# A hybrid decoder trunk: places, ring and order for the weights of the pooling mixer's seven half products

## The chip, the core and the metric

The kernel runs on one core of one Trainium2 chip. A core has five engines that run side by side, each through its own list of instructions in order: TensorE (PE; its weight loads are shown apart as PEld), VectorE (DVE), ScalarE (ACT), GpSimd (POOL) and SyncE (SP). Here SP issues nearly all plain DMAs, and POOL those that add onto what is already in the target. The metric is the device time of one execution in microseconds (us); times inside an execution are counted from the start of its span.

## What is computed

Two residual layers over 512 tokens of width 1024, each a token mixer and a SwiGLU feed-forward network (FFN), and a last norm. Layer 0 mixes by causal pooling, layer 1 by dilated windowed attention. The change touches the pooling mixer, above all its output projection by `w_out`:

```python
def pool_mixer(h, w_in, w_group, scale, w_out):
    u = einsum('bsd,de->bse', h, w_in)                    # 512x1024 by 1024x1024
    outs = [(cumsum(u_g) - lagged by w) / count - u_g for u_g, w in the 4 groups]
    z = einsum('bsgc,gce->bsge', outs, w_group) * scale   # four 256x256
    return einsum('bsd,de->bse', z, w_out)                # 1024x1024

x = x + pool_mixer(rmsnorm(x), ...)
x = x + swiglu(rmsnorm(x), ...)
```

## The kernel before

**Precision.** Each operand is held as two parts, `hi` and `lo`. ACT casts (`hi`), DVE subtracts (`lo`, "the rest"), and a product is three matmuls: hi by hi, hi by lo, lo by hi.

**Weights.** All weights stand in one `queue` in the order of use. `weights(i, ...)` loads raw tiles ahead (512 KB each, `wraw`, five in turn) and casts some items ahead into a ring of five pairs `whi`/`wlo` (pool `wspl`, `RING = 5`). An item with `"pool": "b"` gets its pair (`bhi`/`blo`) from another pool, which is opened only after the windows of the mixer, in memory that the `poolu` tiles held until then. An item with `"sums"` is loaded into a tile of the pool `s` (`sraw`), opened at the same place.

**The seven half products.** Where `SEVEN_OUT[0]` is on (it is; `SEVEN_OUT[1]`, for attention, is off), the output projection is one level of Strassen-Winograd: seven products of half matrices in place of eight. Product `i` takes a left operand `u` (quarters of `z`, or sums and differences of them, split into hi and lo by the class `Left`) and a right one, a quarter of `w_out` or a sum of quarters. It has 24 matmuls of 512 columns, ordered by weight tile (z = 0, 1), then token block (t = 0, 1), then chunk (c = 0, 1), three for each. Sums of weights are made by POOL's adding DMAs: the tile for product 1 gets two quarters, then a third is added for product 2, then a fourth for product 5, each after the cast before it has read the tile. `SEVEN` is the order in which they run: 0, 1, 2, 5, 4, 3, 6. Products 0, 2, 4 and 6 accumulate in the PSUM pair `p`, 1 and 5 in `r`, 3 in `q`, and `flush` adds a finished sum into the stream `x` on DVE.

**Around them.** `group_products(0)` and `(1)` make `z`, and ACT evicts their banks into `raw` (L744). The second half runs between product 0 and product 1 (`after_first`). `Left.behind` is called after a product and makes left operands of later ones. `norm.square`, `norm.gained` and `norm.prepare` make the normed rows of the FFN, `turned_rows` transposes the first 128-row blocks on PE (L401), and then product 6 runs, t = 0 first. The FFN starts with products `("one", 0, 0)`, `(0, 3)`, `(1, 0)`, `(1, 3)`, then i = 1 and 2 for both groups; their weights with i = 1, 2, 5 are sums in `vraw` tiles. `late` makes its `t` operands from the last token blocks.

**Order.** PE's order is that of the code. For the other engines a scheduler orders the recorded instructions by its own costs; blocks marked `high_priority(URGENT)` go first. `issue_after` ties an instruction behind another. SP and POOL keep the order of the code too. Each list is fixed when the kernel is built, so an instruction that waits holds all that stand behind it on its engine.

Of the kernel before, what the change touches and what calls it, by code (L numbers as in the profile page):

```python
# [17 lines left out]
P = 128  # L18
# [52 lines left out]
SEVEN = (0, 1, 2, 5, 4, 3, 6)  # L71
# [7 lines left out]
def trunk_kernel(ctx: ExitStack, tc: tile.TileContext, x_in, xT, gam, gains, consts, ident_d, w0, wT, w1, wv, w_down, out):  # L79
# [49 lines left out]
    def load(i):  # L129
# [27 lines left out]
    def weights(i, split_ahead=4, load_ahead=5, held=0):  # L157

        load_ahead = queue[i].get("ahead", load_ahead)
        for n in range(loaded["w"], min(len(queue), i + load_ahead)):  # L160
# [5 lines left out]
        load_sums()  # L166
        while len(ready) < min(loaded["w"], i + split_ahead):
# [36 lines left out]
    j_in.append([enqueue(w0[i], (2, S)) for i in range(4, 8)])  # L204
    w_out, wo = (rows_of(wT[i]) for i in range(2))

    def enqueue_seven(w, order, then=None):
# [295 lines left out]
    class Left:  # L503
# [6 lines left out]
        def split(self, u, src, ks=(slice(0, 4),)):  # L510
            hi, lo = self.places[u]
            for k in ks:
                split(hi[:, k, :], lo[:, k, :], src[:, k, :])
# [33 lines left out]
        def reserve(self):  # L547

            if 4 not in self.places:
                self.places[4] = [  # L550
                    wspl.tile([P, 1024], F32R, name=name).rearrange("p (k s) -> p k s", k=4) for name in ("whi", "wlo")
                ]

    def seven_projection(js, left, norm, shift, p, r, q, tps, after_first, keep):
# [5 lines left out]
        def operands(i):  # L560
            return [weights(j, split_ahead=6, held=z + (i in (4, 3, 6))) for z, j in enumerate(js[i])]

        def products(i, ws, ts=range(2)):
            hi, lo = left.places[(0, 1, 2, 3, 6, 5, 4)[i]]
            places = [(z, t, c) for z in range(2) for t in ts for c in range(2)]
# [16 lines left out]
        def product(i):  # L582
# [1061 lines left out]
```

## Time and profile before

| | us |
|---|---|
| three runs before | 1007.15, 1008.66, 1009.75 (median 1008.66) |
| the profiled execution, its own time | 1008.38 |
| its span, first to last instruction | 1006.6 |
| mean granted clock of TensorE in it | 0.987 |
| product 0 starts | 63.06 |
| product 6 ends and the FFN starts | 130.23 |

Rows of the timeline read: start, duration, engine, source line, operation, output <- inputs, shape, and in brackets the idle time of the engine just before and what ended it. Rows of waits read: who waited for whom, us in total, times, longest. Rows of stretches give busy time by engine. "mm", "early" and "pair" are PSUM banks.

### The profile page before, as it was taken

To read this page: it belongs to the slowest core of one execution; us is meant where nothing else is said; L and a number is where in the kernel's file an instruction comes from. 1 tells how busy PE (TensorE), PEld (TensorE's weight loads), DVE (VectorE), ACT (ScalarE), POOL (GpSimd) and SP (SyncE) were. 2 spreads that over 40 slices of the span, in tenths; PEclk is the share of its full clock that TensorE was granted. 3 is DMA by queue.
4 is the path that set the end of the run, shared out by engine and by line. 5 is a ranking of instruction groups with operands and counts; after the bars stand their busy time and mean duration, and the time that the engine had idled before them with its cause. 6 is when DMAs were issued, how large, how long until landed. Compare 5 with 4: busy or idle time off the path is not lost.

```text
span 1006.6 us, 15596 instructions
## 1 busy us (share of the span) xinstructions
PE 976.2 (97%) x6004; PEld 863.9 (86%) x6004; DVE 800.3 (80%) x1097; ACT 589.9 (59%) x919; POOL 134.3 (13%) x132
## 2 busy tenths in 40 slices
PE   9996998899999999999999999999999999999997
PEld 7874788898898899888888899889998898899886
DVE  6445987989798888879887747669989788888877
ACT  5544856564675566657354454447655566566655
POOL 0101101001001110110212104100001101111110
PEclk9997998999999999999999999999999999999999
DMA  9745777648946987665332128924757966897652
GB/s 334 215 127 87 214 153 214 146 127 205 255 118 174 252 203 189 148 157 186 100 103 61 53 79 245 216 46 149 195 139 199 246 169 147 225 235 179 156 129 112
DMA packets 82186, 168.24 MB, mean 167 GB/s; under 512 B 6256, under 2 KB 6640, under 8 KB 82112
## 3 DMA queue, kind: packets, MB, share of 16 engines
q1 hardware_dynamic: 59088, 123.09, 37.4%
q0 software_dynamic: 22736, 43.89, 25.6%
q8 instruction: 47, 0.77, 0.3%
q14 instruction: 27, 0.22, 0.1%
q10 hardware_dynamic: 288, 0.27, 0.1%
HBM read 165.09 MB, written 2.13 MB: 166 GB/s over the span
## 4 chain that ended last, share of the span: by engine, by line
PE 80%; ACT 0%; DVE 0%; issue 0%; ACTq 0%
PE pair L888 31%; PE pair L1032 21%; PE mm L299 4%; PE mm L301 3%; PE mm L300 3%; PE pair L914 3%; PE p L914 2%; PE r L914 1%; PE mm L1485 1%; PE mm L1486 1%; PE mm L1487 1%; PE mm L460 1%; PE mm L461 1%; PE mm L462 1%; PE mm L1532 1%; PE mm L914 1%
## 5 line engine op out<-in xcount | busy, mean ns | idle before, releaser
L183 DVE TENSOR_TENSOR wlo<-wraw,whi 128x1024 fp32r<-128x1024 f32 (+2 forms) x190 | 221.8, 1172 | 56.4 <-ACT whi L179 56.0
L179 ACT CAST whi<-wraw 128x1024 fp32r<-128x1024 f32 (+2 forms) x189 | 183.9, 979 | 133.8 <-PE pair L888 28.6
L179 ACT CAST whi<-vraw 128x1024 fp32r<-128x1024 f32 (+1 forms) x108 | 105.2, 979 | 118.3 <-DVE vraw L185 39.9
L183 DVE TENSOR_TENSOR wlo<-vraw,whi 128x1024 fp32r<-128x1024 f32 (+1 forms) x108 | 121.5, 1133 | 46.4 <-ACT whi L179 46.3
L888 PE MATMUL pair<-h,whi 128*128 128x512 f32 (+1 forms) x640 | 143.2, 349 | 0.0
L888 PEld LDWEIGHTS pair<-h,whi 128*128 128x128 f32 x640 | 109.1, 189 | 13.4
L888 PE MATMUL pair<-t,whi 128*128 128x512 f32 (+1 forms) x512 | 110.6, 337 | 0.0
L1032 PE MATMUL pair<-whi,u_hi 128*128 128x512 f32 (+1 forms) x284 | 109.9, 387 | 0.0
L1032 PE MATMUL pair<-wlo,u_hi 128*128 128x512 f32 (+1 forms) x284 | 109.9, 387 | 0.0
L1032 PE MATMUL pair<-whi,u_lo 128*128 128x512 f32 (+1 forms) x284 | 109.7, 386 | 0.0
L888 PEld LDWEIGHTS pair<-t,whi 128*128 128x128 f32 x512 | 86.0, 190 | 8.4
L888 PE MATMUL pair<-h,wlo 128*128 128x256 f32 x512 | 89.2, 281 | 0.0
L888 PEld LDWEIGHTS pair<-h,wlo 128*128 128x128 f32 x512 | 76.1, 188 | 4.2
L185 DVE TENSOR_TENSOR vraw<-vraw,wraw 128x1024 f32<-128x1024 f32 (+1 forms) x66 | 75.2, 1139 | 0.7
L888 PE MATMUL pair<-t,wlo 128*128 128x256 f32 x384 | 71.9, 282 | 0.0
L144 POOL DMA_DIRECT2D wraw<-w x22 | 26.5, 1206 | 323.5 <-DMA wraw<-w 144.8
L299 PE MATMUL mm<-h,whi 128*128 128x512 f32 (+1 forms) x176 | 64.3, 365 | 0.0
L301 PE MATMUL mm<-h,wlo 128*128 128x512 f32 (+1 forms) x176 | 63.4, 360 | 0.0
L300 PE MATMUL mm<-h,whi 128*128 128x512 f32 (+1 forms) x176 | 63.4, 360 | 0.0
L1032 PEld LDWEIGHTS pair<-whi,u_lo 128*128 128x128 f32 x284 | 53.3, 188 | 10.9
L1032 PEld LDWEIGHTS pair<-whi,u_hi 128*128 128x128 f32 x284 | 53.4, 188 | 10.4
L1032 PEld LDWEIGHTS pair<-wlo,u_hi 128*128 128x128 f32 x284 | 53.4, 188 | 10.2
(413 smaller groups left out, 2063.8 us busy)
## 6 DMA issues: line engine op xcount, KB each, us to landing
wraw<-w SPq DMA_DIRECT2D x116, 512.0 KB, 4.5
wraw<-w_down SPq DMA_DIRECT2D x32, 512.0 KB, 4.1
vraw<-w SPq DMA_DIRECT2D x22, 512.0 KB, 5.0
wraw<-w POOLq DMA_DIRECT2D x22, 512.0 KB, 6.9
vraw<-w POOLq DMA_DIRECT2D x22, 512.0 KB, 9.2
wraw<-wT SPq DMA_DIRECT2D x16, 512.0 KB, 4.2
vraw<-w_down POOLq DMA_DIRECT2D x12, 512.0 KB, 7.1
wraw<-w_down SPq DMA_DIRECT2D x24, 256.0 KB, 3.3
```

Of the source, the lines that this page charges most:

```text
L144: nc.gpsimd.dma_start(dst, more, accum_op=ALU.add)
L179: nc.scalar.copy(hi[:, :n], raw[:, :n])
L183: nc.vector.tensor_sub(lo[:, :n], raw[:, :n], hi[:, :n].bitcast(F32))
L185: nc.vector.tensor_add(raws[into][:, :n], raws[into][:, :n], raws[more][:, :n])
L299: nc.tensor.matmul(ps, lhsT=whi, rhs=xhi, start=first, stop=False, **kw)
L300: nc.tensor.matmul(ps, lhsT=whi, rhs=xlo, start=False, stop=False, **kw)
L301: nc.tensor.matmul(ps, lhsT=wlo, rhs=xhi, start=False, stop=last, **kw)
L460: nc.tensor.matmul(ps, lhsT=xhi, rhs=w[0][:, k, :], start=first, stop=False)
L461: nc.tensor.matmul(ps, lhsT=xhi, rhs=w[1][:, k, :], start=False, stop=False)
L888: mat = lambda o, w, m, **kw: nc.tensor.matmul(o, lhsT=w, rhs=m, skip_group_check=True, **kw)
L914: nc.tensor.matmul(ps[:, g, :], lhsT=w[:, g, c, :], rhs=right[:, z, c, :], start=i in (0, 1, 3) and g + c + k == 0, stop=c == 3 and k == 2 ...
L1032: nc.tensor.matmul(acc(t), lhsT=u, rhs=w, start=first, stop=n == len(places) - 1, skip_group_check=True)
```

## The change

Five things, all of them in the first mixer.

1. The two tiles for weight sums (`sum0`, `sum1`) are allocated with the mixer's first tiles. `load_until` loads them and, with them, all items to the end of product 1, right after the window bands are loaded. Behind them the load-ahead goes on, so that product 4's raw tiles and their adding DMAs are early too.
2. The weights of products 0 and 1 with z = 1 take the ring, not pool `b`.
3. The casts of the weights of products 2 and 5 are tied behind the last eviction of the group products (`cast_behind`); `group_products(1)` casts no more than its own weights ahead.
4. The order becomes 0, 1, 2, 4, 5, 3, 6. `behind` makes left operands in another sequence, only its first step stays URGENT, and `reserve` goes. Norm squares of the second half now come before product 5, those of the first before product 3.
5. The transposes move from ahead of product 6 to behind its first six matmuls, and the rests of the turned rows with them.

```diff
-SEVEN = (0, 1, 2, 5, 4, 3, 6)
+SEVEN = (0, 1, 2, 4, 5, 3, 6)
...
-            raw = pools["s"].tile([P, 1024], F32, name="sraw")
+            raw = pools["s"]()
...
+    def load_until(end):
+
+        for n in range(loaded["w"], min(len(queue), end)):
             if queue[n].get("sums") and "s" not in pools:
                 break
             if queue[n]["kind"] == "w":
                 load(n)
             loaded["w"] = n + 1
         load_sums()
...
-                item = dict(kind="w" if src else "sum", shape=(2, S), rows=True, ahead=8, **({"pool": "b"} if z else {}))
+                item = dict(kind="w" if src else "sum", shape=(2, S), rows=True, ahead=8, **({"pool": "b"} if z and i > 1 else {}))
...
-            with tc.high_priority(URGENT):
-                if i is None:
+            if i is None:
+                with tc.high_priority(URGENT):
                     self.next_sum(FIRST)
                     self.split(2, self.spare)
-                    self.split(5, more[:, :, FIRST])
-                    nc.vector.tensor_sub(t[:, :, FIRST], more[:, :, FIRST], t[:, :, FIRST])
-                elif i == 0:
-                    self.split(6, t[:, :, FIRST])
-                elif i == 1:
-                    self.split(3, more[:, :, SECOND])
-                    self.next_sum(SECOND)
-                elif i == 4:
-                    self.split(4, self.spare)
...
+            elif i == 0:
+                nc.vector.tensor_sub(t[:, :, FIRST], more[:, :, FIRST], t[:, :, FIRST])
+                self.split(6, t[:, :, FIRST])
+            elif i == 1:
+                self.split(5, more[:, :, FIRST])
+                self.next_sum(SECOND)
+            elif i == 2:
+                self.split(3, more[:, :, SECOND])
+                self.split(4, self.spare)
...
-        product(5)
+        product(4)
+        ws = operands(5)
+        for b in range(2):
+            norm.square(b, 1)
+            norm.gained(b, 1)
+        product(5, ws)
         for b in range(2):
             norm.square(b, 0)
             norm.gained(b, 0)
-        left.reserve()
-        product(4)
-        for b in range(2):
-            norm.square(b, 1)
-            norm.gained(b, 1)
             norm.prepare(b)
         product(3)
         for t in range(2):
             norm.square(2 + t, 0, q[t])
-        rests = turned_rows(norm, shift, list(enumerate(tps())))
         ws = operands(6)
-        rests()
+        products(6, ws, (0,), (0,))
+        turned_rows(norm, shift, list(enumerate(tps())))()
+        products(6, ws, (0,), (1,))
         for t in range(2):
+            if t:
+                products(6, ws, (1,))
             norm.gained(2 + t, 0)
-            products(6, ws, (t,))
             flush(6, t)
...
+            sums = [pm.tile([P, 1024], F32, name=f"sum{i}") for i in range(2)]
...
+            pools["s"] = lambda: sums.pop(0)
+            load_until(j_out[1][-1] + 1)
...
-            whi, wlo = weights(j_grp[half])
+            whi, wlo = weights(j_grp[half], 1 if half else 4)
...
-                group_products(1, early)
+                made = group_products(1, early)
+                for i in (2, 5):
+                    for j in j_out[i]:
+                        queue[j]["cast_behind"] = made.ins
                 left.second()
                 left.behind(None)
```

The diff also changes lines of the attention layer that act only with `SEVEN_OUT[1]` on, and gives one item of `j_in` a load-ahead of 8.

Three places of the fixed order, each before and after. First ACT around the evictions of the group products; `early` and `mm` are PSUM banks, `wraw_304` (before) and `wraw_306` (after) hold product 0's weights with z = 1, `sraw` and `sum` the weight sums. Before, from the split of the last window bank on:

```order
L422 CAST p_hi_109<-early3_105 128x512
L179 CAST bhi_610<-wraw_304 128x1024
L179 CAST whi_618<-sraw_604 128x1024
L744 ACTIVATE raw1_107<-early0_102,g_sb_76 128x512
L179 CAST bhi_623<-sraw_607 128x1024
L744 ACTIVATE raw1_107<-early1_103,g_sb_76 128x512
```

In the changed kernel these casts stand earlier, around the first half's evictions:

```order
L183 CAST whi_528<-wraw_300 128x1024
L183 CAST whi_532<-wraw_306 128x1024
L183 CAST whi_536<-wraw_308 128x1024
L705 ACTIVATE u_hi_116<-mm_501,r4_341 128x512
L183 CAST whi_618<-sum0_109 128x1024
L747 ACTIVATE raw0_106<-mm_540,g_sb_76 128x512
L747 ACTIVATE raw0_106<-mm_548,g_sb_76 128x512
L426 CAST h_74<-raw0_106 128x512
L747 ACTIVATE raw0_106<-mm_558,g_sb_76 128x512
L183 CAST whi_623<-sum1_110 128x1024
L747 ACTIVATE raw0_106<-mm_566,g_sb_76 128x512
```

The casts of products 0 and 1 have moved from ahead of and among the evictions of the second group half (`raw1`) to ahead of and among those of the first (`raw0`), and they go to `whi`, not `bhi`.

Second, DVE from the last eviction of the group products to the rests of product 2's weights (`wlo_629`, `blo_634` before; `wlo_695`, `blo_700` after). `x<-x,mm` is a flush of product 1. Before:

```order
L526 SCALAR_TENSOR_TENSOR spare_sum_108<-spare_sum_108,raw1_107 128x1024
L423 TENSOR_TENSOR h_74<-raw1_107,h_74 128x1024
L538 TENSOR_TENSOR raw0_106<-raw1_107,raw0_106 128x4x256
L423 TENSOR_TENSOR h_74<-spare_sum_108,h_74 128x1024
L580 TENSOR_TENSOR x_72<-x_72,mm_602 128x512
L423 TENSOR_TENSOR p_lo_110<-raw0_106,p_hi_109 128x1024
L580 TENSOR_TENSOR x_72<-x_72,mm_603 128x512
L423 TENSOR_TENSOR p_lo_110<-raw1_107,p_hi_109 128x1024
L526 SCALAR_TENSOR_TENSOR spare_sum_108<-spare_sum_108,raw1_107 128x1024
L183 TENSOR_TENSOR wlo_629<-sraw_604,whi_628 128x1024
L183 TENSOR_TENSOR blo_634<-sraw_607,bhi_633 128x1024
```

And in the changed kernel, to the flush of product 2 (`x<-mm,x`):

```order
L530 SCALAR_TENSOR_TENSOR spare_sum_108<-spare_sum_108,raw1_107 128x1024
L542 TENSOR_TENSOR raw0_106<-raw1_107,raw0_106 128x4x256
L187 TENSOR_TENSOR wlo_695<-sum0_109,whi_694 128x1024
L427 TENSOR_TENSOR h_74<-spare_sum_108,h_74 128x1024
L577 TENSOR_TENSOR x_72<-x_72,mm_613 128x512
L577 TENSOR_TENSOR x_72<-x_72,mm_614 128x512
L427 TENSOR_TENSOR p_lo_112<-raw0_106,p_hi_111 128x1024
L187 TENSOR_TENSOR blo_700<-sum1_110,bhi_699 128x1024
L187 TENSOR_TENSOR wlo_705<-wraw_615,whi_704 128x1024
L187 TENSOR_TENSOR blo_709<-wraw_628,bhi_708 128x1024
L575 TENSOR_TENSOR x_72<-mm_611,x_72 128x512
L575 TENSOR_TENSOR x_72<-mm_612,x_72 128x512
```

Product 2's first rest has moved from the tenth place to the third, its second from the eleventh to the eighth; the flush of product 2, which product 4 on the same bank needs, stands behind both rests of product 4's weights.

Third, DVE near the end of the stage, around the rest of product 6's second weights (`blo_837` before, `blo_830` after), whose raw tile is the next one that SP loads for the FFN ahead of the `vraw` tiles. `x<-x,mm` is the flush of product 4, `x<-early,x` that of product 3. Before:

```order
L183 TENSOR_TENSOR blo_793<-wraw_752,bhi_792 128x1024
L578 TENSOR_TENSOR x_72<-mm_603,x_72 128x512
L368 TENSOR_TENSOR even_rows_593<-x_72,gain_595 128x512
L361 TENSOR_SCALAR ss_594<-ss_594 128x1
L183 TENSOR_TENSOR wlo_799<-wraw_758,whi_798 128x1024
L368 TENSOR_TENSOR odd_rows_81<-x_72,gain_595 128x512
L361 TENSOR_SCALAR ss_594<-ss_594 128x1
L183 TENSOR_TENSOR blo_837<-wraw_790,bhi_836 128x1024
L580 TENSOR_TENSOR x_72<-x_72,mm_600 128x512
```

And in the changed kernel:

```order
L187 TENSOR_TENSOR wlo_798<-wraw_753,whi_797 128x1024
L379 TENSOR_TENSOR v1_884<-ss_608 128x1
L380 RECIPROCAL r1_886<-s1_885 128x1
L381 TENSOR_SCALAR v1_872<-v1_872,r1_874,s1_873 128x1
L381 TENSOR_SCALAR v1_884<-v1_884,r1_886,s1_885 128x1
L382 RECIPROCAL r1_874<-v1_872 128x1
L575 TENSOR_TENSOR x_72<-early0_102,x_72 128x512
L382 RECIPROCAL r1_886<-v1_884 128x1
L575 TENSOR_TENSOR x_72<-early1_103,x_72 128x512
L187 TENSOR_TENSOR blo_830<-wraw_789,bhi_829 128x1024
```

The rest of product 6's second weights has moved from ahead of the flush two products before it to behind the flush of product 3, the last before it.

More of the change, by code (lines that the diff above doesn't have):

```diff
@@ L166, in weights @@
         load_sums()
+    def weights(i, split_ahead=4, load_ahead=5, held=0):
+        load_ahead = queue[i].get("ahead", load_ahead)
+        load_until(i + load_ahead)
         while len(ready) < min(loaded["w"], i + split_ahead):
@@ L203, in trunk_kernel @@
     j_in = [[enqueue(w0[0][:, i * S : (i + 1) * S], (1, S)) for i in range(2)] + [enqueue(w0[i], (2, S)) for i in range(1, 4)]]
-    j_in.append([enqueue(w0[i], (2, S)) for i in range(4, 8)])
+    j_in.append([enqueue(w0[i], (2, S), **({"ahead": 8} if i == 7 else {})) for i in range(4, 8)])
     w_out, wo = (rows_of(wT[i]) for i in range(2))
@@ L512, in split @@
             for k in ks:
[L513 removed]
+                self.cast = split(hi[:, k, :], lo[:, k, :], src[:, k, :])[0]
         def first(self, k):
@@ L560, in operands, with products @@
         def operands(i):
-            return [weights(j, split_ahead=6, held=z + (i in (4, 3, 6))) for z, j in enumerate(js[i])]
-        def products(i, ws, ts=range(2)):
+            return [weights(j, split_ahead=6, held=z) for z, j in enumerate(js[i])]
+        def products(i, ws, ts=range(2), zs=range(2)):
             hi, lo = left.places[(0, 1, 2, 3, 6, 5, 4)[i]]
-            places = [(z, t, c) for z in range(2) for t in ts for c in range(2)]
+            places = [(z, t, c) for z in zs for t in ts for c in range(2)]
             for z, t, c in places:
@@ L580, in flush, with product @@
                     nc.vector.tensor_sub(at, at, accs[i][t])
-        def product(i):
-            products(i, operands(i))
+        def product(i, ws=None):
+            products(i, ws or operands(i))
             for t in range(2):
@@ L743, in group_products @@
                         with tc.high_priority(URGENT):
-                            nc.scalar.activation(raw[half][:, 2 * gg + m, :], ps, AF.Copy, scale=sc)
+                            made = nc.scalar.activation(raw[half][:, 2 * gg + m, :], ps, AF.Copy, scale=sc)
                             if half == 0 and m == 1:
@@ L751, in group_products @@
                     )
+            return SEVEN_OUT[0] and made
         quarters = lambda t: t.rearrange("p a b -> p (a b)").rearrange("p (u k s) -> p u k s", u=4, k=4)
@@ L1182, in trunk_kernel @@
         at = 8 * SPAN
-        angles = aw.tile([P, D], F32, name="angles", bufs=1)
+        seven = SEVEN_OUT[1]
+        angles = (ap if seven else aw).tile([P, D], F32, name="angles", bufs=1)
         cosr, sinr = (angles[:, cs] for cs in COLS)
@@ L1501, in trunk_kernel @@
         mp = actx.enter_context(tc.tile_pool(name="merged", bufs=1, reuse_waits="tile"))
-        seven = SEVEN_OUT[1]
         pools["b"] = actx.enter_context(tc.tile_pool(name="wob", bufs=3 if seven else 4, reuse_waits="tile"))
+        two = mp.tile([P, D], F32, name="even_rows")
+        factors = ring + [two[:, cs] for cs in COLS]
         if seven:
-            pools["s"] = actx.enter_context(tc.tile_pool(name="wos", bufs=2, reuse_waits="tile"))
-        two = mp.tile([P, D], F32, name="even_rows")
-        of_heads = [weights_of(t, to) for t, to in enumerate(ring + [two[:, cs] for cs in COLS])]
+            factors.append(masks[:, :S])
+        of_heads = [weights_of(t, to) for t, to in enumerate(factors)]
         m_hi, m_lo = h_hi, h_lo
@@ L1515, in trunk_kernel @@
             places.update({6: places[0], 3: places[1]})
+            places[4] = [mp.tile([P, 4, 256], F32R, name=name) for name in ("u4_hi", "u4_lo")]
             left = Left(raw, fours(flat_p, 8 * S, 256), places)
```

18 lines of the change are left out of this document (8 added, 10 removed).

## The prediction

> **What bounds the kernel now.** I read the page's busy times first, then the stretches of the stage that changes, then who waits for whom in it, then the timeline of each engine.
>
> ```profile
> span 1006.6 us, 15596 instructions
> PE 976.2 (97%) x6004; PEld 863.9 (86%) x6004; DVE 800.3 (80%) x1097; ACT 589.9 (59%) x919; POOL 134.3 (13%) x132
> ```
>
> TensorE (PE) is busy 97% of the span, so a gain must come from the few stretches where it isn't. Those that matter are the half products of the pooling mixer. Below is one row for each: PE, PEld, DVE, ACT and POOL busy, then the granted clock, DMA share and GB/s.
>
> ```profile
> 63.06:73.03 9.97, 7.71 (x27) 5.66 (x27) 5.70 (x8) 3.75 (x6) 2.44 (x2) 0.83 0.69 169
> 73.03:78.50 5.47, 5.47 (x26) 4.50 (x24) 1.23 (x1) 1.64 (x2) 1.02 (x1) 1.00 0.88 172
> 78.50:85.06 6.56, 5.91 (x25) 4.24 (x23) 2.52 (x3) 5.12 (x8) 1.38 (x2) 1.00 0.64 92
> 85.06:102.10 17.04, 8.41 (x25) 6.46 (x25) 11.72 (x12) 6.99 (x8) 2.44 (x2) 0.70 0.49 84
> 102.10:109.14 7.04, 6.06 (x25) 4.35 (x24) 7.04 (x8) 6.34 (x7) 0.00 (x0) 1.00 0.37 97
> 109.14:114.58 5.44, 5.44 (x25) 4.51 (x24) 5.44 (x10) 3.38 (x6) 0.00 (x0) 1.00 0.86 284
> 114.58:120.03 5.45, 5.45 (x25) 4.32 (x23) 5.43 (x15) 3.68 (x9) 0.00 (x0) 1.00 0.84 276
> 120.03:130.23 10.20, 8.70 (x57) 6.91 (x57) 8.69 (x17) 6.36 (x13) 4.86 (x4) 0.83 0.91 214
> ```
>
> In order these are product 0, the group products, then products 1, 2, 5, 4, 3, and transposes with 6. Two products run without a wait at full clock in 5.44 and 5.45, so seven of them and the group products need 43.6 us. The stage takes 67.2. The other 23.6 are waits, half clock and transposes.
>
> ```profile
> PE mm L571 <- DVE wlo L183: 6.5, 2, 6.0
> ...
> 68.81 0.71 PE L571 MATMUL mm<-blo,h 128*128 128x512 f32 x1 [1.29 <-DVE blo L183]
> 69.31 1.06 PE L571 MATMUL mm<-bhi,h 128*128 128x512 f32 x2
> ...
> 121.35 0.71 PE L401 MATMUL early<-ident,even_rows 64*128 64x64 f32 x16 [1.17 <-ACT even_rows L387]
> ...
> 65.90 1.07 ACT L179 CAST bhi<-wraw 128x1024 fp32r<-128x1024 f32 x1
> 74.81 1.05 ACT L179 CAST whi<-sraw 128x1024 fp32r<-128x1024 f32 x1 [7.85 <-DMA sraw<-wT]
> ...
> 79.90 1.05 ACT L179 CAST bhi<-sraw 128x1024 fp32r<-128x1024 f32 x1 [3.46 <-DMA sraw<-wT]
> ...
> 83.05 0.69 ACT L744 ACTIVATE raw<-early,g_sb 128x512 f32<-128x512 f32 x1
> ...
> 84.72 1.04 ACT L422 CAST p_hi<-raw 128x1024 fp32r<-128x1024 f32 x1
> 85.67 1.04 ACT L422 CAST h<-spare_sum 128x1024 fp32r<-128x1024 f32 x1
> ...
> 109.33 0.64 ACT L359 ACTIVATE even_rows<-x 128x512 f32<-128x512 f32 x1 [0.35 <-DVE x L578]
> ```
>
> Product 0 waits because its second weights are cast only at 65.90. Product 2 waits because ACT stands at 79.90 for a weight sum's DMA with three evictions of the group products queued behind it. The last eviction starts at 83.05, and only behind it can DVE work (casts of 128x1024 on ACT start 0.95 apart, from 84.72 to 85.67):
>
> ```profile
> 63.40 0.68 DVE L423 TENSOR_TENSOR h<-raw,h 128x512 fp32r<-128x512 f32 x1
> ...
> 65.74 1.88 DVE L423 TENSOR_TENSOR p_lo<-early,p_hi 128x512 fp32r<-128x512 f32 x3
> ...
> 83.77 1.23 DVE L526 SCALAR_TENSOR_TENSOR spare_sum<-spare_sum,raw 128x1024 f32<-128x1024 f32 x1 [1.56 <-ACT raw L744]
> ...
> 92.92 1.22 DVE L183 TENSOR_TENSOR wlo<-sraw,whi 128x1024 fp32r<-128x1024 f32 x1
> 94.06 1.22 DVE L183 TENSOR_TENSOR blo<-sraw,bhi 128x1024 fp32r<-128x1024 f32 x1
> ...
> 104.01 1.28 DVE L578 TENSOR_TENSOR x<-mm,x 128x512 f32<-128x512 f32 x2
> ```
>
> DVE starts at 83.77 and has product 2's first rest done at 92.92 + 1.22 = 94.14, behind nine other operations. Starts lie 1.14 apart for 128x1024 (92.92 to 94.06), and a pair of 128x512 takes 1.28 (0.6 to 0.65 each).
>
> **Part by part, to the end of product 6.** I lay the changed order on these durations. Product 0 starts at 63.06 as before.
>
> Both weights of products 0 and 1 are now cast in the ring. ACT and DVE get the two weights of product 1 among the first half of the group products, and what stands behind the second comes about 1.5 later: product 0's last left rest (63.40 + 0.68) ends at 65.6, and PE needs it at 66.2. Product 0: 9.97 to 5.45, **-4.5**. The last `p_lo` (65.74 + 1.88) comes at 69.1, and the group products need it at 63.06 + 5.45 + 0.9 = 69.4. Product 1's operands are long ready: 6.56 to 5.45, **-1.1**. It ends at 63.06 + 5.45 + 5.47 + 5.45 = 79.4.
>
> The last eviction is now at 74.1 to 74.8. DVE then has four 1.14s (to 79.4), two flushes of product 1 (to 80.7), the rest of operand 6 and then `blo` of product 2, made at 82.95. PE wants that at 82.35: a wait of 0.65 in place of the 6.0 and the smaller ones and half clock. Product 2: 17.04 to 6.1, **-10.9**.
>
> Product 4 now adds straight onto the bank of product 2 and must wait for that flush, which stands behind two weight rests on DVE: 82.95 + 2 x 1.14 + 0.7 = 85.9, against 85.5. So 7.04 becomes 5.8, **-1.2**. Product 5's second sum is issued behind product 2's `blo`, lands at 83.1 + 5.8 = 88.9 (the median of these sums, quoted below), is cast by 90.0 and has its rest at 91.15; PE wants that at 94.2: no wait, **0**.
>
> Product 3 gets worse. On DVE stand, from 91.15: two flushes, a weight rest, a wait of 1.1 for ACT (90.0 + four casts of 0.95, then a square of 0.64 and its sum, to 94.7), two gains, product 3's left rest, a flush, another left rest, a flush, a gain, and only then product 3's `blo`: 91.15 + 1.3 + 1.2 + 1.1 + 1.3 + 1.15 + 0.65 + 1.15 + 0.65 + 0.65 + 1.2 = 101.5. PE wants it at 99.9. With 0.15 for the left rest: 5.45 to 7.2, **+1.8**. Product 3 ends at 104.0.
>
> The transposes now stand behind a quarter of product 6, 1.4 us of cover for the 1.17 they waited. With 2 x 0.7 of transposes and 0.35 of waiting between them, 10.20 becomes 7.2, **-3.0**, half clock not counted. Sum: -4.5 - 1.1 - 10.9 - 1.2 + 1.8 - 3.0 = **-18.9**; product 6 ends near 111.3.
>
> The waits of 0.15 and 1.65 in product 3 could bring half clock: the 9.97 - 7.71 = 2.26 of waiting in product 0 did (two matmuls take 1.06 at 69.31). Those lay with one matmul between them, mine make 1.8 with twelve between, so I take none; with it product 3 would end 1.5 later and the total about 1 us. The Trainium skill ("TensorE: Matmul & The Clock Gate", Part 1) says half rate follows an idle window of about 3.4 us; by that no wait here would bring it, and the sum would stand. The trace's 2.26 us disagrees with so long a window.
>
> **Given back in the FFN's start.** The next rows say what comes after product 6.
>
> ```profile
> 113.41 1.21 DVE L183 TENSOR_TENSOR blo<-wraw,bhi 128x1024 fp32r<-128x1024 f32 x1
> ...
> 115.11 1.49 SPq L142 DMA_DIRECT2D vraw<-w  x3
> ...
> 122.01 1.20 POOL L144 DMA_DIRECT2D wraw<-w  x1 [24.84 <-DMA vraw<-w]
> 123.14 2.52 POOL L144 DMA_DIRECT2D vraw<-w  x2
> ...
> vraw<-w POOLq DMA_DIRECT2D x3, 512.0 KB, 10.5
> ...
> 135.02 1.05 ACT L179 CAST whi<-vraw 128x1024 fp32r<-128x1024 f32 x1
> ...
> 141.08 1.22 DVE L185 TENSOR_TENSOR vraw<-vraw,wraw 128x1024 f32<-128x1024 f32 x1
> ...
> 142.36 16.91 SPq L142 DMA_DIRECT2D wraw<-w  x6
> ...
> 152.58 1.04 ACT L179 CAST whi<-wraw 128x1024 fp32r<-128x1024 f32 x1 [4.90 <-DMA wraw<-w]
> ...
> 154.68 1.30 PE L914 MATMUL p<-t,whi 128*128 128x256 f32 x2 [4.86 <-ACT t L422]
> ```
>
> From 142 to 154.68 a chain decides, not PE: the DVE add at 141.08 frees a raw tile, its load is issued at 142.36, is landed, summed and cast at 152.58, and the cast of `t` behind it on ACT lets PE go at 154.68. And the v weights: SP's loads of them stand behind one that waits for product 6's `blo` (113.41 to 114.6), POOL sums them from 123.14, and the second (issued about 124.4, 10.5 to land) is there at about 135, just when ACT first wants one, without a wait.
>
> That cover goes. Product 6's `blo` was made 15.6 us before product 6 ended; it now stands behind product 3's flushes. From 101.5: a gain 0.65, a weight rest 1.2, 128x1 steps 0.7 (as between 118.2 and 120.0 in the trace of before), two flushes 1.3, itself 1.2: 106.6, only 4.7 before the end. So the v loads move by 114.6 - 106.6 = 8.0, not 18.9. POOL sums from 114.0, the second v sum lands at 127.0, and ACT, whose casts of both v sums now stand ahead of the cast of `h` from `t1r`, waits for it. Then cast 1.0, `h` 0.6, its rest 0.65, the add 1.2: 130.45 in place of 142.3, **-11.85**. The load, sum and casts behind it (142.3 to 154.68 is 12.4) are the same less one copy of 0.5 that moves behind the cast: PE goes at 142.35 in place of 154.68, **-12.3**. PE gets a new wait ahead of the FFN's fifth product too, but this chain ends later than that one.
>
> DVE also gets three weight rests ahead of `t1r` that it had done earlier. They fall into ACT's wait for the v sums, so I cost them at nothing; without that cover they are 3 x 1.14 = 3.4.
>
> Behind 154.68 both kernels hold the same rows in the same order, and PE waits but 3.1 in the next 85 us; I carry -12.3 through and round to **-12.0**. The unknown in it is the landing of the v sums. The mixer's sums landed in 5.8 (median), the v sums, four in a bunch, in 10.5. With 5.8 the second would be there at 115.2 + 1.2 + 5.8 = 122 and the gain 17; with the longest, 11.2, the gain would be 11.3. I take the 10.5, since the changed kernel issues the same bunch.
>
> **Edits at nothing.** The sums and product 4's weights load from 25 to 50 now, and PE covers that:
>
> ```profile
> 30.00:60.00 30.00, 30.00 (x163) 25.84 (x162) 12.59 (x25) 16.47 (x34) 2.52 (x2) 1.00 0.59 153
> 35.21 1.32 POOL L144 DMA_DIRECT2D wraw<-wT  x1 [34.76 <-DVE v L697]
> ...
> DMA to landing us min/median/max: 3.8/5.8/11.2
> ```
>
> PE is fully busy there and DMA 59%. POOL's first sum went out at 35.21; even if each took the longest 11.2 and they ran one after the other, the two that are cast early would be there at 46.4 and 57.6, and ACT wants them at 56.7 and 61.5. Without the cover each microsecond late is one of product 0's start. The attention lines do nothing, as their switch stays off. The flush and copy counts don't change.
>
> The profiled execution took 1008.38 us (1.8 around its span), 0.3 under the median of 1008.66: 1008.4 - 12.0 = **996.4**.
>
> **Rivals.**
> *Full credit:* the v sums land early and the FFN's start moves by the whole stage less the DVE's extra rests, -17 to -17.5: **991**. Against it: the 10.5. For it: fewer other loads may be in flight than at 115.
> *A late sum for product 5:* POOL adds it at 83.1, beside loads freed at 84.1 and 85.2. The longest landing in the row above is 11.2. With it, ACT stands from 87.1 to 94.3, DVE's later rests come 5 us later, product 6's `blo` and the v loads with them: -7, **1001.4**. The Trainium skill ("Trainium Kernel Development and Optimization", Key Constraints) says that DMAs of all queues share the same 16 engines and interleave; by that rule this sum is slowed as well, and the 11.2 agrees with that. Against it: the median of 5.8.
> *No gain:* the early places don't free the casts, or the FFN takes all back: within 3 us of 1008.4. The changed order has the casts ahead of the evictions, so only other waits could do it.
> *Slower:* the casts from the early sums now stand on ACT ahead of the first group evictions and product 0's splits. The second can go at 61.5. If its sum lands later than 61.5 + 12.0 + 3 = 76.5, the kernel is slower by over 3; at 80 it is 1008.4 + 3 + 3.5 = **1015**. Against it: 57.6 at the worst, as worked out.
>
> **Chances and range.** Forecast (992 to 999.5 of its own) 0.70, full credit 0.11, late sum 0.12, no gain 0.04, slower 0.03. 0.3% is 3 us, about what a measurement of this kernel can tell from no change: faster 0.92, same 0.05, slower 0.03, a little of the late sum counted as same. The range reaches over the full credit and the late sum: 990 to 1002.5.
>
> **What would show it.** Product 0 without a wait and at full clock; a first wait of about 0.65 for product 2's `blo`; product 4 waiting under 1 us for a flush; product 3 waiting 1 to 2 us for `blo`; product 6 ending near 111; ACT waiting several us for the v sums near 120 to 127; PE's wait for `t` ending near 142. It is wrong if product 2 still waits for DVE by several us, if ACT stands for a sum between 56 and 92, or if product 6's gain reaches the end unshortened.

## The result, and the profile after

| | before | after |
|---|---|---|
| median of four runs | 1008.41 us | 995.54 us (994.83 to 995.96) |
| ratio to before, 95% interval | | 0.9871 [0.9854, 0.9889] |
| span of the profiled execution | 1006.6 us | 993.1 us |
| product 0's first matmul | 63.06 | 63.49 |
| the FFN's first matmul (product 6 done) | 130.23 | 114.04 |
| PE's first matmul with `t` | 154.68 | 144.82 |
| from there to the end of the span | 851.9 | 848.3 |

The kernel is 12.9 us faster, 1.3%, and the interval is clear of no change; 12.0 was forecast. The page of the profile after, the row to set beside the first one of the prediction:

```profile
span 993.1 us, 15597 instructions
...
PE 973.5 (98%) x6004; PEld 862.8 (87%) x6004; DVE 799.1 (80%) x1097; ACT 588.4 (59%) x919; POOL 134.3 (14%) x132
```

The stretches of the stage, with the columns of the prediction's table (stretch, length, then busy time of PE, PEld, DVE, ACT and POOL, granted clock, DMA share, GB/s). In the new order: product 0, group products, products 1, 2, 4, 5, 3, and 6 with the transposes.

```profile
63.49:69.03 5.54, 5.54 (x26) 4.56 (x26) 5.54 (x8) 3.28 (x6) 1.20 (x1) 1.00 0.75 121
69.03:74.47 5.44, 5.44 (x25) 4.51 (x24) 0.27 (x1) 3.21 (x5) 0.00 (x0) 1.00 0.11 20
74.47:79.91 5.44, 5.44 (x25) 4.51 (x24) 4.51 (x4) 5.24 (x6) 0.66 (x1) 1.00 0.00 0
79.91:86.33 6.42, 5.89 (x25) 4.24 (x23) 6.42 (x8) 4.18 (x6) 1.75 (x2) 1.00 0.61 99
86.33:92.05 5.72, 5.54 (x25) 4.62 (x25) 4.13 (x5) 1.81 (x2) 0.00 (x0) 1.00 1.00 231
92.05:97.49 5.44, 5.44 (x25) 4.50 (x24) 3.56 (x4) 5.39 (x8) 0.00 (x0) 1.00 0.07 26
97.49:107.23 9.74, 7.44 (x25) 5.21 (x24) 9.63 (x21) 4.20 (x11) 0.00 (x0) 0.82 0.32 109
107.23:114.04 6.81, 6.81 (x57) 5.50 (x56) 6.70 (x13) 6.71 (x12) 0.54 (x1) 1.00 0.73 262
```

Only product 3 is far from its 5.44 now: 2.3 of its 9.74 were waits and 2.0 half clock (0.82 over the stretch). PE's waits from 60 to 165, all but one of 0.2 (who waited for whom, us in total, times, longest), say what is left:

```profile
PE r L921 <- ACT h L426: 3.2, 1, 3.2
PE p L921 <- ACT t L426: 3.0, 1, 3.0
PE early L568 <- DVE p_lo L427: 2.0, 1, 2.0
PE mm L397 <- ACT even_rows L391: 1.7, 1, 1.7
PE p L921 <- DVE t L427: 0.7, 2, 0.4
PE mm L568 <- DVE blo L187: 0.5, 1, 0.5
PE early L568 <- DVE blo L187: 0.3, 1, 0.3
PE mm L568 <- DVE x L575: 0.2, 1, 0.2
```

Three of the first four lie in the FFN. From its first matmul to the first with `t` PE needs 19.6 by itself (before: 154.68 less the wait of 4.86 less 130.23); now it takes 144.82 - 114.04 = 30.8. So of the 16.2 that the mixer's end gained, 9.9 are left when `t` starts. ACT's timeline there shows on what PE waits (start, duration, line, operation, and in brackets its idle time and what ended it):

```profile
125.11 1.05 ACT L183 CAST whi<-vraw 128x1024 fp32r<-128x1024 f32 x1 [4.95 <-DMA vraw<-w]
127.62 1.05 ACT L183 CAST whi<-vraw 128x1024 fp32r<-128x1024 f32 x1 [1.46 <-DMA vraw<-w]
128.57 0.62 ACT L426 CAST h<-t1r 128x512 fp32r<-128x512 f32 x1
...
139.22 0.62 ACT L426 CAST t<-t2r 128x512 fp32r<-128x512 f32 x1
143.21 1.04 ACT L183 CAST whi<-wraw 128x1024 fp32r<-128x1024 f32 x1 [3.36 <-DMA wraw<-w]
144.16 0.61 ACT L426 CAST t<-t2r 128x512 fp32r<-128x512 f32 x1
```

ACT stands for the DMAs of two sums of v weights with the cast of `h` behind them, and later for a third sum with the second half of `t` behind it. PE's waits of 3.2 and 3.0 are these two. SP's timeline (the second number is from the first issue of the row to the end of its last) says when those loads go out:

```profile
85.79 23.90 SPq L142 DMA_DIRECT2D wraw<-w  x5
109.75 1.49 SPq L142 DMA_DIRECT2D vraw<-w  x3
```

The v loads stand behind the last of five raw loads, which waits for product 6's `blo` (DVE, 108.04 to 109.26).

### The profile page after: what moved, and what is told of

It reads as the page before. It is cut to its first block, busy times and chain, and to the rows that moved or that the text cites. A ratio compares the mean times of both kernels' runs of the same rounds, so it can differ in the third digit from the quotient of the medians.

```text
span 993.1 us, 15597 instructions
## 1 busy us (share of the span) xinstructions
PE 973.5 (98%) x6004; PEld 862.8 (87%) x6004; DVE 799.1 (80%) x1097; ACT 588.4 (59%) x919; POOL 134.3 (14%) x132
## 4 chain that ended last, share of the span: by engine, by line
PE 91%; DMA 4%; ACT 2%; DVE 2%; issue 0%; SPq 0%; ACTq 0%
PE pair L895 32%; PE pair L1039 21%; PE mm L303 5%; PE mm L305 4%; PE mm L304 4%; PE pair L921 4%; PE p L921 4%; PE early L675 2%; PE r L921 2%; DMA vraw<-w 2%; PE mm L1497 1%; PE mm L1499 1%; PE mm L1498 1%; DMA wraw<-w 1%; DMA sum<-wT 1%; PE early L725 1%
```

## The experiments

Twelve runs in three groups of four. The kernel before took 1005.76, 1005.84 and 1006.83 in them, so times are compared by the ratio to before of the same group. In the table the stage is product 0's first matmul to the FFN's first, "to t" is from there to the first matmul with `t`, and "rest" from there to the end of the span.

| run | stage | to t | rest | ratio to before, 95% interval |
|---|---|---|---|---|
| before | 67.2 | 24.5 | 851.9 | 1 |
| changed | 50.6 | 30.8 | 848.3 | 0.9871 [0.9854, 0.9889] |
| c1, changed again | 50.7 | 30.9 | 848.9 | 0.9874 [0.9858, 0.9891] |
| u1, no ring | 60.7 | 20.0 | 847.8 | 0.9869 [0.9855, 0.9884] |
| u2, no ties | 58.5 | 19.7 | 848.9 | 0.9876 [0.9861, 0.9891] |
| u3, late sums | 60.2 | 20.4 | 847.2 | 0.9886 [0.9870, 0.9903] |
| u4, 5 before 4 | 51.8 | 21.8 | 852.1 | 0.9833 [0.9819, 0.9848] |
| u5, transposes first | 52.2 | 25.0 | 847.4 | 0.9820 [0.9801, 0.9840] |
| e1, v loads first | 50.2 | 28.3 | 848.9 | 0.9854 [0.9839, 0.9869] |
| e2, fourth quarter early | 48.1 | 29.6 | 847.2 | 0.9862 [0.9839, 0.9885] |
| e3, e1 and e2 | 48.1 | 27.1 | 848.0 | 0.9823 [0.9804, 0.9842] |
| e4, v loads before item 1, 3 | 50.4 | 22.4 | 848.7 | 0.9800 [0.9785, 0.9814] |
| x1, e4 without the ring | 60.4 | 21.0 | 847.6 | 0.9867 [0.9852, 0.9881] |
| x2, e4 and e2 | 49.0 | 21.5 | 849.8 | 0.9810 [0.9790, 0.9830] |

### First group: the two places where time was given back

e1. Ahead of the `vraw` loads SP waited for a raw tile (`wraw_1221`) that product 6's `blo` frees. Here that load stands behind them (33 is its item, 40 the third v item):

```diff
-        nc.sync.dma_start(dst, item["src"][0])
+        with tc.issue_after(raws["v"].ins) if i in (33,) and "v" in raws else nullcontext(): dma = nc.sync.dma_start(dst, item["src"][0])
+        if item["kind"] == "v" and i == 40: raws["v"] = dma
```

> The load of the fifth FFN raw tile (wraw_1221) is tied behind the three vraw loads on SP, nothing else is changed. In the changed kernel SP stood for product 6's blo until 109.3 with the vraw loads behind it (109.75 to 110.8), though their own tiles were free. Theory A (the landing of the v sums sets the FFN's start, and SP's order sets the landing): the vraw loads go out near 106.6, 3.1 earlier; ACT's first and second v casts start near 122 and 124.5 instead of 125.1 and 127.6, PE's wait for t ends near 141.7 instead of 144.8; the time falls by 3 to 992.5. Rival R1 (POOL's bunch of adding DMAs is bound by bandwidth, so starting earlier shifts little): the second sum lands within 1 us of 127.6, no change. Rival R2 (wraw_1221 itself is late now): its cast stands at 136.1 and moves back, 996 to 997.

The v loads went out at 105.82, ACT's first two v casts started at 119.44 and 124.48, and `t` at 141.37 (this execution is 0.6 ahead of the changed kernel's when product 0 starts). Apart from the first cast, which came 2.6 earlier, these times are theory A's. By the ratios some 1.7 of the 3 us reached the end; the two intervals overlap, so that this gain by itself is not clear of noise.

e2. The fourth quarter of product 5's weights is added earlier, because product 2's rests come first on DVE:

```diff
-            with tc.issue_after(item["behind"]) if "behind" in item else nullcontext():
+            with tc.issue_after(item["behind"]) if "behind" in item else nullcontext(), tc.high_priority(URGENT) if len(ready) in j_out[2] else nullcontext():
```

> The rests of product 2's two weights get the first priority on DVE, so that they stand right behind the cast and POOL can add the fourth quarter for product 5 some 4 us earlier (at 80 instead of 84.2). Theory A (product 3's waits of 2.0 and 0.3 and its half clock, 97.5 to 107.2, come from product 5's second sum, which landed at 92.1 and not at 88.9 as forecast): the sum lands near 86 to 88, ACT doesn't stand at 88.1 to 92.1, product 3 takes 5.5 to 7.2 instead of 9.74, product 6 ends near 110.5 to 111.5 instead of 114.0, and product 6's blo and the FFN behind it move too: 992 (-3 to -4). Product 4 may lose 0.7, since the rest of its left operand now stands behind a flush. Rival (DVE's own backlog, not the sum, holds product 3): product 3 still takes over 9, 995 to 996.

For the stage theory A holds. These are products 5, 3, and 6 with the transposes of this run, with the columns as above:

```profile
91.71:97.15 5.44, 5.44 (x26) 4.50 (x25) 5.16 (x7) 2.12 (x5) 0.00 (x0) 1.00 0.17 41
97.15:104.33 7.18, 5.75 (x25) 4.42 (x24) 7.18 (x19) 3.60 (x8) 0.00 (x0) 1.00 0.32 112
104.33:111.14 6.81, 6.81 (x58) 5.50 (x56) 6.81 (x12) 6.80 (x13) 0.58 (x1) 1.00 0.87 293
```

Product 3 takes 7.18, with one wait of 1.43 for `blo`, and product 6 ends at 111.14. That is the forecast for the changed kernel (7.2, a wait of 1.65, 111.3), so the late sum accounts for nearly all by which the changed kernel missed it. By the median the time fell by about 1 us and not by 3 to 4, but its four runs lie 5 us apart (989.8 to 995.0), and the profiled one is the fastest. In that one nothing is taken back: "to t" and "rest" in the table are each 1.1 shorter than in the changed kernel, and the span is 5.1 shorter. The mean granted clock is 0.996 in it and 0.992 in the two slowest runs. By an estimate (twice 0.004 of 988) that is some 8 us more at half clock, or 4 us of work. Why they had more of it isn't shown, as only one run has a trace.

e3 has both edits.

> Both edits of the two runs before at once. If product 5's sum and SP's order are two separate terms, their gains add up: near 989 (-6.5). If the second gain comes only out of the same chain (product 6's blo frees the tile for which SP waits), then taking SP's wait away leaves nothing more for the earlier blo to move: near 991 to 992.

The ratio is 0.0048 or 4.8 us under the changed kernel's, between what was expected of two separate terms (6.5) and of one chain (3.5 to 4.5), and the intervals allow either. The traces tell more. Counted from product 0's first matmul, `t` starts 2.8 earlier than in the changed kernel in e1, 3.6 earlier in e2 and 6.1 earlier in e3: at this place the two nearly add up, and the one doesn't replace the other.

e4. The v loads stand ahead of the FFN's fourth item too (28). The last two edits keep this item from being loaded in the mixer and load the v tiles as soon as their pool is open:

```diff
+        with tc.issue_after(raws["v"].ins) if i in (28, 33) and "v" in raws else nullcontext(): dma = nc.sync.dma_start(dst, item["src"][0])
+        if item["kind"] == "v" and i == 40: raws["v"] = dma
...
-        load_ahead = queue[i].get("ahead", load_ahead)
+        load_ahead = min(queue[i].get("ahead", load_ahead), 28 - i if i < 25 else 99)
...
-            pools["v"] = open_pool("ffv", V_TILES)
+            pools["v"] = open_pool("ffv", V_TILES); load_sums()
```

> As the first of these, and the load of the FFN's fourth item (weights 3 of group 1) stands behind the v loads too, so that these go out as soon as their memory is free, near 104.7. By the new list ACT casts the operands from t1r ahead of the v sums. Theory A: v sums land 5 us earlier than in the changed kernel, PE's wait of 3.2 for h (132.7) is gone, the wait for t ends near 136 to 139: 987 to 990. Rival (the fourth item's weights, now loaded some 2 us later and cast behind the norm's rows, hold PE at its first use near 126.5; or the raw tile of the chain to t is still late): a new wait there and 992 to 996.

ACT's timeline of this run at the place that was shown of the changed kernel:

```profile
121.68 0.62 ACT L426 CAST h<-t1r 128x512 fp32r<-128x512 f32 x1 [1.40 <-DVE t1r L1009]
...
122.68 2.00 ACT L183 CAST whi<-vraw 128x1024 fp32r<-128x1024 f32 x2
...
133.42 0.62 ACT L426 CAST t<-t2r 128x512 fp32r<-128x512 f32 x1
...
134.92 0.62 ACT L426 CAST t<-t2r 128x512 fp32r<-128x512 f32 x1
137.96 1.06 ACT L183 CAST whi<-wraw 128x1024 fp32r<-128x1024 f32 x1 [2.42 <-DMA wraw<-w]
```

`h` no longer stands behind the v sums, and both halves of `t` stand ahead of the cast that waits for a sum. PE's wait for `h` is gone, the one for `t` is 1.2, and `t` starts at 135.60. This version beats both kernels: 985.87 us, 2.0% under before. But two things changed at once, the loads (out at 103.88 instead of 109.75) and ACT's list.

### Second group and u5: each part of the change undone by itself

u1, the ring:

```diff
-                item = dict(kind="w" if src else "sum", shape=(2, S), rows=True, ahead=8, **({"pool": "b"} if z and i > 1 else {}))
+                item = dict(kind="w" if src else "sum", shape=(2, S), rows=True, ahead=8, **({"pool": "b"} if z else {}))
```

> Undoes part 2 alone: the weights of products 0 and 1 with z = 1 get their pairs from pool b again, which opens when the windows are done (63.5). Theory (the ring gives product 0 its 4.5): ACT casts product 0's second weights only behind the four p_hi splits, near 66.5 to 67.5, and their rest comes near 68 to 69, where PE wants them at 66.2: product 0 takes 8.5 to 10 instead of 5.5, the rest of the stage moves with it, 997.5 to 1000 on a chip where the changed kernel takes 995.5 (ratio to before 0.989 to 0.992, against 0.987). Rival (the early sums alone had freed ACT, the ring adds nothing, or the FFN takes it back): product 0 under 6.5 or the time within 1 us of the changed kernel's.

u2, the ties:

```diff
-                for i in (2, 5):
-                    for j in j_out[i]:
-                        queue[j]["cast_behind"] = made.ins
```

> Undoes the ties of part 3 alone: the casts of the weights of products 2 and 5 may stand ahead of the last eviction of the group products, and by the new list one for product 5 stands between the evictions. Theory (an ACT that stands for a sum's DMA holds evictions, as in the kernel before): that sum can be added only after product 2's rest, lands near 78 to 80, and the last evictions, wanted at 73 and 75, come at 80 to 81; PE waits about 5 to 6 for product 2's left operand; 1000 to 1002 (ratio 0.992 to 0.995). Rival (the early sums made the ties superfluous): within 1 us of the changed kernel (0.987).

u3, the early places:

```diff
-            sums = [pm.tile([P, 1024], F32, name=f"sum{i}") for i in range(2)]
...
-            raw = pools["s"]()
+            raw = pools["s"].tile([P, 1024], F32, name="sraw")
...
-            pools["s"] = lambda: sums.pop(0)
-            load_until(j_out[1][-1] + 1)
...
         norm = Norm(0, px.tile([P, D], F32, name="even_rows"))
         if SEVEN_OUT[0]:
+            pools["s"] = open_pool("pools", 2)
```

> Undoes part 1 alone: the two tiles for sums come from a pool opened after the windows, as before, with ring, ties and order kept. Theory (the places from the outset are the base of all the rest): the sums for product 1 can be loaded only from 63.5, land near 74 to 76, and by the new list stand among the evictions on ACT; product 1 waits 2 to 4, product 2's and product 5's additions come 6 to 10 later each: product 6 ends 8 to 13 later, 1002 to 1008 (ratio 0.994 to 1.0). Rival (ring and order carry the gain): 995.5 to 999 (0.987 to 0.991).

In the stage the three theories hold in kind, but u1 and u2 cost more than they said. PE's longest wait in u1, which is in product 0, by the view of waits:

```profile
PE mm L568 <- ACT bhi L183: 4.9, 1, 4.9
```

Product 0 waits again for its second weights. It takes 13.95, not 8.5 to 10, as a second wait of 1.0 and half clock are added, and the stage takes 10.2 longer. ACT's timeline in u2 shows the evictions (`raw<-early`) held behind casts of sums whose DMAs aren't there:

```profile
75.29 0.70 ACT L747 ACTIVATE raw<-early,g_sb 128x512 f32<-128x512 f32 x1
78.75 1.05 ACT L183 CAST bhi<-sum 128x1024 fp32r<-128x1024 f32 x1 [2.77 <-DMA sum<-wT]
79.71 0.68 ACT L747 ACTIVATE raw<-early,g_sb 128x512 f32<-128x512 f32 x1
80.29 0.59 ACT L592 COPY early<-mm 128x512 f32<-128x512 f32 x1
84.58 1.04 ACT L183 CAST whi<-sum 128x1024 fp32r<-128x1024 f32 x1 [3.70 <-DMA sum<-wT]
85.53 0.68 ACT L747 ACTIVATE raw<-early,g_sb 128x512 f32<-128x512 f32 x1
```

The last eviction comes at 85.53 instead of 74.67 (80 to 81 was expected) and PE waits 9.1 for product 2's left operand; the stage takes 8.0 longer. In u3 PE waits in products 1, 2 and 4, and the stage takes 9.7 longer. And yet none of the three is slower than the changed kernel by more than 1.5 us: "to t" falls from 30.8 to 20, which is PE's own 19.6 and a little. On the time the rivals were right, though only u1's names the FFN as the reason. `t` can start at the later of two chains: PE's own work (FFN's start plus 19.6), and the loads, sums and casts of the FFN, which in the changed kernel end at 144.8. For u1, u2 and u3 the first gives 143.0, 141.6 and 142.8; measured are 143.4, 141.7 and 143.5. The changed kernel's own is at 133.6, 11.2 under what it takes.

But these three runs differ from the changed kernel in more than the stage. The scheduler's list for ACT in the FFN is another one in each of them: both halves of `t` stand ahead of the cast that waits for the third sum. This is u1:

```profile
141.72 1.14 ACT L426 CAST t<-t2r 128x512 fp32r<-128x512 f32 x2
143.75 1.05 ACT L183 CAST whi<-wraw 128x1024 fp32r<-128x1024 f32 x1 [0.89 <-DMA wraw<-w]
```

In u2 and u3 that cast starts at 145.07 and 144.38. In the changed kernel `t` starts 1.6 after it (143.21 to 144.82). So with the changed kernel's list `t` would have started, by an estimate from these rows, at about 145.4, 146.7 and 146.0 in u1, u2 and u3: 0.5 to 1.9 later than in the changed kernel, where it did start 1.3 to 3.1 earlier. That these parts could be left out without a loss of time is in part the work of this other list, and no run undoes a part with the list kept.

u4, the swap of products 4 and 5:

```diff
-SEVEN = (0, 1, 2, 4, 5, 3, 6)
+SEVEN = (0, 1, 2, 5, 4, 3, 6)
...
-        product(4)
-        ws = operands(5)
+        product(5)
+        ws = operands(4)
         for b in range(2):
-            norm.square(b, 1)
-            norm.gained(b, 1)
-        product(5, ws)
+            norm.square(b, 0)
+            norm.gained(b, 0)
+        product(4, ws)
         for b in range(2):
-            norm.square(b, 0)
-            norm.gained(b, 0)
+            norm.square(b, 1)
+            norm.gained(b, 1)
             norm.prepare(b)
```

> Undoes the swap of part 4: products run 0, 1, 2, 5, 4, 3, 6 again, with the norm's squares in the order of before. Theory (product 4 covers the landing of product 5's sums): product 5's sums, issued near 79 and 84, land near 85 and 91; PE wants the second weights near 88.6 and waits 4.5 to 6 for them; product 4 then runs without a wait; product 6 ends 3 to 5 later and the FFN with it: 998 to 1000 (ratio 0.990 to 0.992). Rival (the order of the two doesn't matter, as product 3 pays for the late sum in either order): within 1 us (0.987).

u5, the transposes:

```diff
-        ws = operands(6)
-        products(6, ws, (0,), (0,))
-        turned_rows(norm, shift, list(enumerate(tps())))()
-        products(6, ws, (0,), (1,))
-        for t in range(2):
-            if t:
-                products(6, ws, (1,))
-            norm.gained(2 + t, 0)
+        rests = turned_rows(norm, shift, list(enumerate(tps())))
+        ws = operands(6)
+        rests()
+        for t in range(2):
+            norm.gained(2 + t, 0)
+            products(6, ws, (t,))
```

> Undoes part 5 alone: the transposes and their rests stand ahead of product 6 again. In the mixer: a wait of 1 to 1.8 for the last normed rows, the transposes without cover and half clock behind them, 1 to 3 in all. Theory (the chain from the v loads decides, and product 6's end has 10 to spare): the time is that of the changed kernel within 1 us. Rival (product 6's end still counts): 1 to 3 slower.

Both expectations fell. In u4 product 5 didn't wait for its sums but 3.0 for its left operand's rest and 0.7 for a weight's, and product 3, which then had its operands in time, ran without a wait: the stage became 1.3 longer. In u5 it became 1.6 longer. Both kernels are about 4 to 5 us faster than the changed one, as "to t" is 9.0 and 5.8 shorter. ACT's timeline in u5:

```profile
126.05 1.05 ACT L183 CAST whi<-vraw 128x1024 fp32r<-128x1024 f32 x1 [1.82 <-DMA vraw<-w]
127.01 0.61 ACT L426 CAST h<-t1r 128x512 fp32r<-128x512 f32 x1
...
129.26 1.05 ACT L183 CAST whi<-vraw 128x1024 fp32r<-128x1024 f32 x1 [1.15 <-DMA vraw<-w]
...
139.21 1.14 ACT L426 CAST t<-t2r 128x512 fp32r<-128x512 f32 x2
140.79 1.05 ACT L183 CAST whi<-wraw 128x1024 fp32r<-128x1024 f32 x1 [0.45 <-DMA wraw<-w]
```

The v loads went out at 110.76, no earlier than in the changed kernel. But the scheduler's list for ACT, which the edit shifts far behind its own place, has the first cast of `h` behind one v sum, not two, and both halves of `t` ahead of the cast that waits. PE doesn't wait for ACT's cast of `t` any more. u4's list has `t` at the same place. So all five lists with a part undone have it there, and the whole change, as the kernel before, has not.

### Third group: do the mixer's microseconds count?

c1 is the changed kernel once more.

> The changed kernel once more, unchanged, so that the runs of this group have it beside them on the same chip. Ratio to before 0.985 to 0.989; product 0 to the FFN's first matmul 50.5, from there to the first matmul with t 30.8.

x1 undoes the ring in e4.

> The ring undone (as in the run where product 0 waited 4.9 and the mixer took 10.2 longer with no change of the time) together with the v loads ahead of the FFN's fourth item (as in the run that gained 6.9). Theory (the FFN's first matmul with t starts at the later of two chains: the v loads, and PE's own work, which needs 19.4 to 20.0 from the FFN's first matmul; with the v loads early PE's own work is the later one, so the mixer's time shows again): the FFN starts near 123.4, t is reached near 143, some 7 later than with the ring, and the time is the changed kernel's or a little under it (ratio 0.986 to 0.988). Rival (what the mixer loses without the ring is taken in elsewhere, whatever the v loads do): the time of the run with the v loads early alone, ratio 0.980 to 0.982.

The time is 993.69 and the ratio that of the changed kernel; `t` starts at 144.3, PE's own chain gives 123.3 + 19.6 = 142.9. Where the FFN's chain is short, the 10 us of the ring are worth 7. The run isn't quite clean: the v loads went out at 108.43 here, since in this list the tile ahead of them came free later; but PE's own chain alone forbids e4's 135.6.

x2 has e2 and e4.

> The two edits that each did well, together on the changed kernel: the v loads ahead of the FFN's fourth item, and product 2's rests first on DVE, so that product 5's sum is early. Theory: the FFN starts near 111.2 (2.3 earlier), the v loads go out near 102, t is reached near 133 to 134 and the time is 1.5 to 3 under that of the v loads early alone: ratio 0.977 to 0.979. Rival (t's chain keeps to the v loads' landing, which moves by under 1): ratio 0.980.

The ratio of 0.9810 isn't under e4's 0.9800, as the rival said. Its reason doesn't hold in the trace, though: `t` starts 1.9 earlier than in e4, at 133.69, where the theory had it, and 1.1 is lost again behind it. The profiled run, 985.25, is the fastest of four that reach to 989.81; the trace doesn't show what slowed the others.

## Why the prediction was right, and where it was not

The range and the direction were right, and most steps of the working too. That the total came so near is partly luck, as the last points of this part show.

**Products 0, 1, 2 and 4 and the group products** came out as worked out: 5.54 (5.45 forecast), 5.44 (5.45), the wait for product 2's `blo` 0.53 (0.65), product 4's for a flush 0.18 (0.35). u1, u2 and u3 show the causes in the stage: without the ring product 0 waits, without the ties and without the early places the evictions or the sums come late.

**Product 5's second sum** was the step of the stage that failed: "lands at 83.1 + 5.8 = 88.9". It was issued at 84.16 and landed at 92.1, in 7.9. The stretch of product 4 above has DMA at a share of 1.00: two raw tiles that SP loaded from 84.66 on ran beside it. PE didn't wait for it in product 5, but ACT and DVE did, and handed it on to product 3: 9.74 instead of 7.2. This was the rival of the late sum, in a milder form. One of the prediction's own signs of being wrong came with it, ACT standing for a sum between 56 and 92: it stood 2.24 for the first (to 85.19) and 3.97 for the second (to 92.10). And product 3 waited 2.0 for its left operand's rest and 0.3 for `blo`, where 0.15 and 1.65 were forecast. e2, with the sum in time, gives the forecast's 7.2 and 111.3 to 0.2.

**Half clock in product 3**, costed at nothing, came, and the prediction had priced it at 1.5. By c1 it cost next to nothing here: there product 3 ran at full clock and took 9.75 against 9.74, since PE waited 2.3 and 1.3 in place of 2.0 and 0.3. What DVE makes last sets the end of product 3, and most of the 2.0 of half clock lay in time in which PE would have waited.

**The transposes and product 6** took 6.81 (7.2).

**The start of the FFN.** The forecast moved the v loads by 8.0; they moved by 115.1 - 109.75 = 5.4, as product 6's `blo` came 2.7 late. The second v sum landed at 127.6 all the same (127.0 forecast), since POOL's first v addition followed the first v load by 4.8 (114.51 - 109.75) where it had been 8.0 (123.14 - 115.11). The DVE addition that frees the next raw tile ended at 129.83 + 1.22 = 131.05 (130.45). The sum behind it was cast at 143.21, 12.1 after its load was issued, where before it had been 10.2: the addition into it landed 8.0 after its issue, before 6.2. Why it was slower isn't shown. So `t` at 144.82 instead of 142.35. The mechanism is the forecast one, and its gain is 2.5 smaller, most of it by this mis-sized landing.

**"Behind 154.68 both kernels hold the same rows in the same order"** was wrong, to the kernel's favour. Before, ACT's copy `keep` stood behind a v cast that waited for DVE, and PE's matmuls behind it:

```profile
188.18 1.04 ACT L179 CAST whi<-vraw 128x1024 fp32r<-128x1024 f32 x1 [2.87 <-DVE vraw L185]
189.13 0.58 ACT L966 COPY keep<-pair 128x512 f32<-128x512 f32 x1
...
189.76 0.50 PE L914 MATMUL pair<-t,whi 128*128 128x256 f32 x2 [3.06 <-ACT keep L966]
```

After, by the same view:

```profile
174.65 0.58 ACT L973 COPY keep<-pair 128x512 f32<-128x512 f32 x1
...
177.79 1.05 ACT L183 CAST whi<-vraw 128x1024 fp32r<-128x1024 f32 x1 [1.06 <-DVE vraw L189]
```

The two have changed places, and PE's wait of 3.1 is gone. The rest is 3.6 shorter. Not all of that need be the 3.1: in the 30 us behind the start of `t` the granted clock was half for 6.4 us before and for 3.4 after. In c1 it was half for 6.1, and the rest is 3.0 shorter. So 9.9 and 3.6 make the 13.5 by which the span fell: a give-back that was forecast 2.5 too small and a gain that wasn't seen nearly cancel, and this is luck.

**What the sum of parts hides.** The prediction added the stage's terms and then took 6.6 back. The runs show a later of two chains. u1, u2 and u3 lose 8 to 10 of the stage's 16 us without a change of the time that the intervals show. Most of these lie under the FFN's chain, and what was left was made up by the other list of ACT, by the estimate above. u4 and u5 are 4 to 5 us faster than the whole change with a longer stage. The order of ACT in the FFN is the difference that the traces show; it isn't a price of parts 4 and 5, as u1, u2 and u3 have both parts and the better list too.

**A correction to the part on the kernel.** It says that SP keeps the order of the code. By the tile numbers it doesn't: `wraw_1221` is issued ahead of `vraw_1059`, and e1 had to tie it. The scheduler orders SP's DMAs too.

**What stays open.** In e4 the loads and the list of ACT change together. e1 moves the loads with the list of ACT unchanged and gains some 2 us, u5 changes the list with the loads unmoved and gains some 5, which speaks for the list as the larger part. A tie of `t`'s casts alone, in the changed kernel, would show it and tell which of the rows did it, and this wasn't run. u4 loses 3.8 behind `t`: a new wait of 2.5 for `t` and 6.8 us of half clock (145.3 to 152.2, twice the changed kernel's 3.4) would make about 4.2. e2, x2 and u5 spread over 3.6 to 5.2 us from run to run. In e2 the slower runs have the lower granted clock; in u5 they don't (990.56 at 0.998), and the cause stays open.

## What to carry to other kernels

Before adding up what a stage gains, work out each chain into the next stage (here PE's own work, and the loads, sums and casts of the next weights): the time follows the later one. x1 shows it best: the ring is worth 10 us in the stage and, once the loads are early, 7 in the time. Where a scheduler lays out the lists, compare the lists of every engine well behind the edit too, of every run that undoes a part above all, or its time is the price of the part and of another list at once. Look for a cast that stands for a DMA ahead of one on which PE waits: u5, without such a row ahead of `t`, is some 5 us faster, though its stage is 1.6 longer. Price an adding DMA that other loads run beside by its slow landing (7.9 and 8.0 here) and not by its median (5.8).

## What the runs showed of the hardware

Half clock after a wait is partly a matter of chance. In the profile of the changed kernel a wait of 1.99 at 100.10 was followed by it from 101.6 to 104.8; in its second profile (c1) one of 2.33 at the same matmul, with 1.34 four microseconds later, was not. In u1 the clock was half from 69.1 to 76.0, beginning inside a wait of 4.88 that ended at 70.54. In e1 and e4 it was half from 100.1 and 100.8, behind waits of 1.91 and 1.86. By the granted clock, the stretches of half clock between 64 and 164 us lasted 3.4, 6.8 or 10.2 in all fourteen traces (3.4 in the changed kernel from 101.6, 6.8 in u1, 10.2 before from 89.4). The Trainium skill ("TensorE: Matmul & The Clock Gate", Part 1) says that the windows of 3.4 us run free of the kernel; the lengths and the chance agree with that, while waits well under its idle window of 3.4 us brought half clock here.
